# x loaded first from two queues, squares summed in pairs on TensorE, and the first block in halves

## The chip, the cores and the metric

The kernel runs on one NeuronCore of one Trainium2 chip. The metric is device time in microseconds (us), the median of three runs. The engines are TensorE (PE in the rows; PEld is its weight load), VectorE (DVE), ScalarE (ACT), GpSimd (POOL) and SyncE (SP), which here only issues transfers. SP's and ACT's transfers go through two queues, q1 and q10 in the rows, to the core's 16 DMA engines.

## The reference

One layer of a diffusion backbone on 256 prompt tokens and 1024 latent tokens of width 1024. Cut to what lies around the change:

```python
def rmsnorm(x, g):
    xf = x.astype(jnp.float32)
    r = lax.rsqrt(jnp.mean(xf * xf, axis=-1, keepdims=True) + EPS)
    return (xf * r).astype(x.dtype) * g

mod_ctx = (jax.nn.silu(c_ctx)[None] @ w_ada[i] + b_ada[i]).reshape(1, 1, N_MOD, D_MODEL)
mod_lat = (jax.nn.silu(c) @ w_ada[i] + b_ada[i]).reshape(c.shape[0], 1, N_MOD, D_MODEL)
...
h = rmsnorm(x, g_norm1) * (1.0 + scale_m) + shift_m
proj = h @ w_in
```

Behind that come a short convolution and a state-space mixer, an output projection, a second norm and a gated feed-forward block with a 3x3 convolution, and a final norm. All of it is in float32.

## The kernel before

Everything is held channel-major: x is 8 tiles of 128 channels (KT = 8), by 256 prompt columns (TP) and 1024 latent columns (TS). A float32 product of the projections is made of three fp32r products of a high and a low part (`hi`, `lo`; `whi`, `wlo`), which ScalarE and GpSimd or VectorE split.

The stage in question is the beginning, up to the first projection. SyncE issues the small constants (`sm`, `cst`, `rows`), then two prompt tiles `xp` (512 KB each, in pieces of 1 KB) and eight latent tiles `xs` (512 KB each, in pieces of 4 KB; they appear in the rows as `bcs` for k under 4 and as `x` for the others). ScalarE squares each tile, VectorE adds the squares up into one tile (`accp` for the prompt, `acc_s` for the latent tokens, both `bc` in the rows), and a matmul with a 128x128 tile of ones (`ones`) sums over the partitions into `pr_p` and `pr_s` (`yp` and `sa` in the rows). ScalarE makes the reciprocal roots `rp` and `rs` of them as exp(-0.5 ln(.)).

Meanwhile `ada_block(k)` computes shift and scale of the norm for the channels of tile k: a load of 1 MB of `w_ad1` into half of the buffer `xq` (`xs<-in_w_ad` in the rows), eight column-tiled matmuls with the silu of the conditioning (`sc`), a copy by ScalarE, two transposes, and three small VectorE instructions that end in `aff`. The loop over k then loads a weight block (`w_l`), calls `ada_block(k + 1)`, scales x (`stt(x, x, aff, rs)`), makes `hi` on ScalarE and `lo` on VectorE, and does twelve matmuls of 512 columns for the two projection blocks that are computed within the loop (`acc<-h` in the rows). The prompt's tiles are multiplied by `rp` and turned into `hp_hi` and `hp_lo` beside it.

The order on each engine is not the order of the code: a scheduler arranges the instructions of each engine by its own estimates, within the data dependencies, and `after(a, b)` adds an order by hand. A tile with a tag and a number of buffers (`T(pool, shape, tag, bufs)`) waits for the release of the buffer that it reuses; transfers share eight completion semaphores a queue's issuer waits on in turn.

Of the kernel before, what the change touches and what calls it, by code (L numbers as in the profile page):

```python
# [9 lines left out]
ALU = mybir.AluOpType  # L10
# [3 lines left out]
P = 128  # L14
# [41 lines left out]
def body(nc, tc, A):  # L56
    cnt = [0]

    def T(pool, shape, tag, bufs, dt=F32):
        cnt[0] += 1  # L60
        return pool.tile(list(shape), dt, tag=tag, bufs=bufs, name=f"{tag}_{cnt[0]}")
# [27 lines left out]

    sm = T(con, [P, SMW], "sm", 1)  # L90
    wff0, wff1 = SMO["wff"]
    dma(sm[:, wff1:], A["sm"][:, wff1:])
    dma(sm[:, 0:wff0], A["sm"][:, 0:wff0])
# [25 lines left out]
    g_hs, hsp = open_pool("hsp", side="right")  # L119
    g_cv, cv = open_pool("cv", side="right")  # L120
    g_xy, xy = open_pool("xy", side="right")
    g_sd, sd = open_pool("sd")
    g_w3, w3 = open_pool("w3")
    wx = [w3]
    g_nrm, nrm = open_pool("nrm")
# [13 lines left out]
    def psa():  # L139
        return T(ps, [P, 512], "sa", 3)  # L140
# [101 lines left out]
    xT = A["xT"]  # L242

    xp = [T(cv, [P, 4, TP], "xl", 2) for _ in range(2)]
    for q in range(2):
        dma(xp[q], xT[:, 4 * q:4 * q + 4, 0:TP])
# [9 lines left out]
    xs = [T(sd, [P, TS], "bcs", 4) if k < 4 else T(nrm, [P, TS], "x", 4) for k in range(KT)]  # L256
    acc_s = T(sd, [P, TS], "bc", 4)
    for k in range(KT):
        dma(xs[k], xT[:, k, TP:TT])
        q = T(cv, [P, TS], "cv", 4) if k else acc_s  # L260
        sq = act(q, xs[k], AF.Square)
        if k:
            tt(acc_s, acc_s, q, ALU.add)
    pr_s = [psa(), psa()]
    for i in range(2):
        nc.tensor.matmul(pr_s[i], ones, acc_s[:, i * 512:(i + 1) * 512], start=True, stop=True)
    tab = lnexp_table(sq)
    rp = T(cv, [P, TP], "cv", 4)
    rs = T(cv, [P, TS], "cv", 4)
    for r, a, b, src in ((rp, 0, TP, pr_p[:, 0:TP]), (rs, 0, 512, pr_s[0]), (rs, 512, TS, pr_s[1])):  # L270
        after(act(r[:, a:b], src, AF.Ln, scale=1.0 / D, bias=epsc), tab)
        act(r[:, a:b], r[:, a:b], AF.Exp, scale=-0.5)
# [43 lines left out]
    ada_block(0)  # L316
    for k in range(KT):
# [8 lines left out]
        stt(x, x, aff[:, 0, k, 1:2], rs, ALU.mult, ALU.mult)  # L326
        hi, lo = [T(hsp, [P, TS], "h", 16, F32R) for _ in range(2)]
        act(hi, x, AF.Identity, bias=col(0, k, 1))
# [11 lines left out]
        if i == 0:  # L340
            tt(xp[q], xp[q], rp.unsqueeze(1).broadcast_to([P, 4, TP]), ALU.mult)
# [995 lines left out]
```

## Time and profile before

| | |
|---|---|
| median of 3 runs | 1554.84 us (1553.34 to 1555.62) |
| the profiled run | 1553.6 us, its span 1551.8 us |
| TensorE busy | 1507.0 us, 97% of the span, 8724 matmuls |
| VectorE, ScalarE, GpSimd busy | 70%, 42%, 33% |
| mean granted TensorE clock | 0.996 of full speed |
| moved by DMA | 187.79 MB, 121 GB/s over the span |

The span runs from the first to the last instruction of the profiled execution; the time of a run lies about 2 us above it. A busy share is a mean over the whole span. The stage that the change touches is the first 75 us of it, and there the shares are others than in the table; the rows below are from this stage.

### The profile page before, as it was taken

Reading aid. Unit: us, or ns where it says so; the run is one execution under the profiler, and the core shown is the slowest. Engines: PE = TensorE matmul, PEld = TensorE weight load, DVE = VectorE, ACT = ScalarE, POOL = GpSimd, SP = SyncE. Lnnn points to the kernel's source line nnn. Section 1 sums busy time; section 2 is a strip of 40 time slices with the busy share of each in tenths; the row PEclk is TensorE's granted clock in tenths of the full one; section 3 lists DMA queues with packets and bytes.
Section 4 is the critical chain, followed back from the end, with each engine's and each line's share of the span. In section 5 each row is a group of like instructions: output and inputs, shape, how many; then the busy total and the mean of one; then the engine's idle time right before and its main releaser. Section 6 shows DMA issues by size and latency. Waiting matters only on the chain. (4 is left out here: it accounts for less than half of the span.)

```text
span 1551.8 us, 22546 instructions
## 1 busy us (share of the span) xinstructions
PE 1507.0 (97%) x8724; PEld 1289.1 (83%) x8724; DVE 1092.2 (70%) x1625; ACT 654.1 (42%) x1020; POOL 516.6 (33%) x289
## 2 busy tenths in 40 slices
PE   4999999999999999999999999999999999999997
PEld 2578888878788888888888888888888888888886
DVE  5765345287885467996666697556679978798696
ACT  6545334267775244433233342332334332433333
POOL 0432321111110003333333333333346554545452
PEclk9999999999999999999999999999999999999999
DMA  8635753443435513221222242121433323342221
GB/s 300 240 109 181 247 209 102 129 161 118 151 109 192 202 68 124 75 70 67 74 64 77 75 156 85 52 69 67 144 121 110 105 89 109 107 154 90 96 78 61
DMA packets 90653, 187.79 MB, mean 121 GB/s; under 512 B 9747, under 2 KB 37299, under 8 KB 90547
## 3 DMA queue, kind: packets, MB, share of 16 engines
q1 hardware_dynamic: 84722, 183.22, 35.0%
q10 hardware_dynamic: 5824, 3.15, 0.7%
q8 instruction: 68, 1.11, 0.3%
q14 instruction: 39, 0.31, 0.1%
HBM read 163.70 MB, written 22.63 MB: 120 GB/s over the span
## 5 line engine op out<-in xcount | busy, mean ns | idle before, releaser
L80 DVE SCALAR_TENSOR_TENSOR cc<-acc,sm,cc 128x504 f32<-128x504 f32 (+5 forms) x836 | 545.8, 665 | 111.3 <-ACT cc L1077 53.0
L77 POOL TENSOR_TENSOR wlo<-raw,whi 128x1024 fp32r<-128x1024 f32 (+2 forms) x91 | 212.6, 2336 | 637.8 <-ACT whi L157 554.0
L157 ACT ACTIVATE whi<-raw 128x1024 fp32r<-128x1024 f32 x97 | 102.6, 1057 | 238.4 <-PE acc L168 185.6
L80 DVE SCALAR_TENSOR_TENSOR x<-dn,mod,x 128x288 f32<-128x288 f32 (+2 forms) x176 | 96.1, 547 | 95.0 <-PE dn L170 94.5
L77 POOL TENSOR_TENSOR dlo<-draw,dhi 128x512 fp32r<-128x512 f32 (+1 forms) x88 | 108.8, 1237 | 89.6 <-ACT dhi L1130 89.6
L77 POOL TENSOR_TENSOR wlx<-raw,whx 128x1024 fp32r<-128x1024 f32 (+2 forms) x36 | 84.7, 2352 | 140.5 <-ACT whx L157 132.4
L168 PE MATMUL acc<-ya,whi 128*128 128x512 f32 (+1 forms) x400 | 118.8, 354 | 0.0
L166 PE MATMUL acc<-ya,whi 128*128 128x512 f32 (+1 forms) x400 | 118.7, 354 | 0.0
L170 PE MATMUL acc<-ya,wlo 128*128 128x512 f32 (+1 forms) x400 | 118.6, 354 | 0.0
L168 PE MATMUL acc<-oa,whi 128*128 128x512 f32 (+1 forms) x400 | 118.6, 354 | 0.0
L170 PE MATMUL acc<-oa,wlo 128*128 128x512 f32 (+1 forms) x400 | 118.6, 354 | 0.0
L166 PE MATMUL acc<-oa,whi 128*128 128x512 f32 (+1 forms) x400 | 118.2, 353 | 0.0
L166 PE MATMUL dn<-yb,dhi 128*128 128x288 f32 (+2 forms) x352 | 110.1, 313 | 5.6 <-DVE x L80 4.4
L168 PE MATMUL dn<-yb,dhi 128*128 128x288 f32 (+2 forms) x352 | 109.6, 311 | 0.8 <-POOL yb L77 0.8
L170 PE MATMUL dn<-yb,dlo 128*128 128x288 f32 (+2 forms) x352 | 109.4, 311 | 0.0
L166 PE MATMUL acc<-h,whi 128*128 128x512 f32 x336 | 108.0, 403 | 0.0
L170 PE MATMUL acc<-h,wlo 128*128 128x512 f32 x336 | 104.9, 394 | 0.0
L168 PE MATMUL acc<-h,whi 128*128 128x512 f32 x336 | 104.8, 393 | 0.0
L1130 ACT ACTIVATE dhi<-draw 128x512 fp32r<-128x512 f32 (+1 forms) x88 | 52.9, 602 | 121.3 <-PE dn L168 49.7
L166 PE MATMUL dn<-g,dhi 128*128 128x288 f32 (+2 forms) x304 | 95.1, 313 | 0.0
L168 PE MATMUL dn<-g,dhi 128*128 128x288 f32 (+2 forms) x304 | 94.8, 312 | 0.3 <-POOL g L77 0.3
L170 PE MATMUL dn<-g,dlo 128*128 128x288 f32 (+2 forms) x304 | 94.8, 312 | 0.0
(345 smaller groups left out, 3538.5 us busy)
## 6 DMA issues: line engine op xcount, KB each, us to landing
raw<-in_w_up SPq DMA_DIRECT2D x88, 512.0 KB, 3.3
raw<-in_w_in SPq DMA_DIRECT2D x32, 512.0 KB, 3.3
ws<-in_w_ada SPq DMA_DIRECT2D x64, 256.0 KB, 4.7
draw<-in_w_down SPq DMA_DIRECT2D x64, 256.0 KB, 2.8
xs<-in_w_ad SPq DMA_DIRECT2D x16, 512.0 KB, 4.5
bc<-csds SPq DMA_DIRECT2D x16, 512.0 KB, 3.6
raw<-in_w_out SPq DMA_DIRECT2D x16, 512.0 KB, 3.4
x<-in_xT SPq DMA_DIRECT2D x8, 640.0 KB, 8.1
```

The costliest lines, as they stand in the source:

```text
L77: (eng or V).tensor_tensor(out=out, in0=a, in1=b, op=op)
L80: V.scalar_tensor_tensor(out=out, in0=a, scalar=s, in1=b, op0=op0, op1=op1)
L157: act(hi, raw, AF.Copy)
L166: nc.tensor.matmul(o, wh[:, k, :], rh(k), start=k == 0, stop=False)
L168: nc.tensor.matmul(o, wh[:, k, :], rl(k), start=False, stop=False)
L170: mm = nc.tensor.matmul(o, wl[:, k, :], rh(k), start=False, stop=k == n - 1)
L1130: act(wh, raw, AF.Copy)
```

## The change

x is issued first: the two prompt tiles on ScalarE's queue, three latent tiles on SyncE's, then the part of `sm` with the conditioning, then the other five latent tiles, then the remaining constants. The pools that hold them are opened earlier for this. The squares of the latent tiles are no longer added up into one tile: each odd one is added to the even one ahead of it, and each of the four sums goes to TensorE, which adds them up in `pr_s`. The last pair's matmuls stand in the code behind `ada_block(0)`, with the roots behind them, and `rs` comes ahead of `rp`. In the loop's first turn (k = 0) the scaling of x and `hi` are done in two halves of 512 columns, and the prompt's multiplication by `rp` is put behind the second half.

```diff
--- before.py
+++ after.py
@@ -87,9 +87,25 @@
     g_wst, wst = open_pool("wst")
 
 
+    g_hs, hsp = open_pool("hsp", side="right")
+    g_cv, cv = open_pool("cv", side="right")
+    g_xy, xy = open_pool("xy", side="right")
+    g_sd, sd = open_pool("sd")
+    g_w3, w3 = open_pool("w3")
+    wx = [w3]
+    g_nrm, nrm = open_pool("nrm")
+    xT = A["xT"]
+    xp = [T(cv, [P, 4, TP], "xl", 2) for _ in range(2)]
+    for q in range(2):
+        nc.scalar.dma_start(xp[q], xT[:, 4 * q:4 * q + 4, 0:TP])
+    xs = [T(sd, [P, TS], "bcs", 4) if k < 4 else T(nrm, [P, TS], "x", 4) for k in range(KT)]
+    for k in range(3):
+        dma(xs[k], xT[:, k, TP:TT])
     sm = T(con, [P, SMW], "sm", 1)
     wff0, wff1 = SMO["wff"]
     dma(sm[:, wff1:], A["sm"][:, wff1:])
+    for k in range(3, KT):
+        dma(xs[k], xT[:, k, TP:TT])
     dma(sm[:, 0:wff0], A["sm"][:, 0:wff0])
 
     def smv(n):
@@ -116,13 +132,6 @@
     aff = T(con, [P, 2, KT, 2], "aff", 1)
 
 
-    g_hs, hsp = open_pool("hsp", side="right")
-    g_cv, cv = open_pool("cv", side="right")
-    g_xy, xy = open_pool("xy", side="right")
-    g_sd, sd = open_pool("sd")
-    g_w3, w3 = open_pool("w3")
-    wx = [w3]
-    g_nrm, nrm = open_pool("nrm")
     g_ps, ps = open_pool("ps1", space=PSUM)
 
     def pacc():
@@ -239,11 +248,7 @@
             after(ln, tab)
         return act(out, out, AF.Exp, scale=-0.5)
 
-    xT = A["xT"]
-
-    xp = [T(cv, [P, 4, TP], "xl", 2) for _ in range(2)]
-    for q in range(2):
-        dma(xp[q], xT[:, 4 * q:4 * q + 4, 0:TP])
+
     accp = T(sd, [P, 4, TP], "bc", 4)
     sqp = T(sd, [P, 4, TP], "bc", 4)
     act(accp, xp[0], AF.Square)
@@ -253,23 +258,17 @@
     pr_p = pst()
     for i in range(2):
         nc.tensor.matmul(pr_p[:, 0:TP], ones, accp[:, i], start=i == 0, stop=i == 1)
-    xs = [T(sd, [P, TS], "bcs", 4) if k < 4 else T(nrm, [P, TS], "x", 4) for k in range(KT)]
-    acc_s = T(sd, [P, TS], "bc", 4)
+    pr_s = [psa(), psa()]
     for k in range(KT):
-        dma(xs[k], xT[:, k, TP:TT])
-        q = T(cv, [P, TS], "cv", 4) if k else acc_s
+        q = T(cv, [P, TS], "cv", 4) if k % 2 else T(sd, [P, TS], "bc", 4)
         sq = act(q, xs[k], AF.Square)
-        if k:
-            tt(acc_s, acc_s, q, ALU.add)
-    pr_s = [psa(), psa()]
-    for i in range(2):
-        nc.tensor.matmul(pr_s[i], ones, acc_s[:, i * 512:(i + 1) * 512], start=True, stop=True)
-    tab = lnexp_table(sq)
-    rp = T(cv, [P, TP], "cv", 4)
-    rs = T(cv, [P, TS], "cv", 4)
-    for r, a, b, src in ((rp, 0, TP, pr_p[:, 0:TP]), (rs, 0, 512, pr_s[0]), (rs, 512, TS, pr_s[1])):
-        after(act(r[:, a:b], src, AF.Ln, scale=1.0 / D, bias=epsc), tab)
-        act(r[:, a:b], r[:, a:b], AF.Exp, scale=-0.5)
+        if k % 2 == 0:
+            qe = q
+            continue
+        tt(q, q, qe, ALU.add)
+        if k < KT - 1:
+            for i in range(2):
+                nc.tensor.matmul(pr_s[i], ones, q[:, i * 512:(i + 1) * 512], start=k == 1, stop=False)
     wdt = T(sd, [P, 640], "toks", 1)[:, 0:KT * 32].rearrange("p (k r) -> p k r", r=32)
     dma(wdt, A["w_dt"])
 
@@ -314,6 +313,14 @@
 
     pps = []
     ada_block(0)
+    for i in range(2):
+        nc.tensor.matmul(pr_s[i], ones, q[:, i * 512:(i + 1) * 512], start=False, stop=True)
+    tab = lnexp_table(sq)
+    rp = T(cv, [P, TP], "cv", 4)
+    rs = T(cv, [P, TS], "cv", 4)
+    for r, a, b, src in ((rs, 0, 512, pr_s[0]), (rs, 512, TS, pr_s[1]), (rp, 0, TP, pr_p[:, 0:TP])):
+        after(act(r[:, a:b], src, AF.Ln, scale=1.0 / D, bias=epsc), tab)
+        act(r[:, a:b], r[:, a:b], AF.Exp, scale=-0.5)
     for k in range(KT):
         raw = T(wst, [P, N_LOOP, P], "raw", 2)
         dma(raw, A["w_l"][k])
@@ -323,9 +330,12 @@
         if k < KT - 1:
             ada_block(k + 1)
         x = xs[k]
-        stt(x, x, aff[:, 0, k, 1:2], rs, ALU.mult, ALU.mult)
         hi, lo = [T(hsp, [P, TS], "h", 16, F32R) for _ in range(2)]
-        act(hi, x, AF.Identity, bias=col(0, k, 1))
+        for a in (0, 512) if k == 0 else (0,):
+            b = 512 + a if k == 0 else TS
+            first = V.scalar_tensor_tensor(out=x[:, a:b], in0=x[:, a:b], scalar=aff[:, 0, k, 1:2],
+                                           in1=rs[:, a:b], op0=ALU.mult, op1=ALU.mult)
+            act(hi[:, a:b], x[:, a:b], AF.Identity, bias=col(0, k, 1))
         stt(lo, x, col(0, k, 1), hi.bitcast(F32), ALU.add, ALU.subtract)
         hs_hi.append(hi)
         hs_lo.append(lo)
@@ -338,7 +348,8 @@
                                      start=k == 0 and n == 0, stop=k == KT - 1 and n == 2)
         q, i = k // 4, k % 4
         if i == 0:
-            tt(xp[q], xp[q], rp.unsqueeze(1).broadcast_to([P, 4, TP]), ALU.mult)
+            after(V.tensor_tensor(out=xp[q], in0=xp[q], in1=rp.unsqueeze(1).broadcast_to([P, 4, TP]),
+                                  op=ALU.mult), first)
         act(hp_hi[q][:, i], xp[q][:, i], AF.Identity, scale=aff[:, 0, k, 0:1], bias=col(0, k, 0))
         ts(xp[q][:, i], xp[q][:, i], aff[:, 0, k, 0:1], col(0, k, 0), ALU.mult, ALU.add)
         if k == 3:
```

How the order moves on the engines. On ScalarE, the beginning of the program; `xl` are the prompt tiles, `bcs` and `x` the latent ones, `sc` the silu, the words in brackets what the instruction waits for (`DMAHW` a transfer). Before:

```order
L114 ACT_TABLE_LOAD [waits DMAHW0_49]
L114 ACTIVATE sc_77<-sm_63 128x8x2 [waits DVE_49]
L110 ACT_TABLE_LOAD
L110 ACTIVATE arow_74<-rows_68 40x1 [waits DMAHW3_49]
L249 ACTIVATE bc_107<-xl_103 128x1024 [waits DMAHW4_49]
L250 ACTIVATE bc_108<-xl_104 128x1024 [waits DMAHW5_49]
L261 ACTIVATE bc_124<-bcs_116 128x1024 [waits DMAHW6_49]
L261 ACTIVATE cv_128<-bcs_117 128x1024 [waits DMAHW7_49]
```

and now:

```order
L100 DMA xl_81<-in_xT 128x4x256
L100 DMA xl_82<-in_xT 128x4x256
L254 ACT_TABLE_LOAD
L254 ACTIVATE bc_123<-xl_81 128x1024 [waits DMAHW0_49]
L255 ACTIVATE bc_124<-xl_82 128x1024 [waits DMAHW2_49]
L264 ACTIVATE bc_134<-bcs_85 128x1024 [waits DMAHW1_49]
L130 ACT_TABLE_LOAD [waits DMAHW5_49]
L130 ACTIVATE sc_115<-sm_96 128x8x2 [waits DVE_49]
L264 ACTIVATE cv_136<-bcs_86 128x1024 [waits DMAHW3_49]
L264 ACTIVATE bc_141<-bcs_87 128x1024 [waits DMAHW4_49]
```

The silu with its table load has moved from the front to behind the third square, and the prompt tiles' loads are on this engine.

On TensorE, from its first instruction to the transposes of block 0; `sa<-bc,ones` and `sa<-cv,ones` are the latent sums, `sa<-xs,sc` the modulation's matmuls. Before:

```order
L266 MATMUL sa_155<-bc_124,ones_70 128x512 [waits DVE_49]
L266 MATMUL sa_156<-bc_124,ones_70 128x512
L292 MATMUL sa_177<-xs_174,sc_77 32x256 [waits DMAHW7_49,Activation_49]
L292 MATMUL sa_177<-xs_174,sc_77 32x256 x3
L292 MATMUL sa_177<-xs_174,sc_77 32x256 [waits DMAHW0_49]
L292 MATMUL sa_177<-xs_174,sc_77 32x256 x3
L298 MATMUL yp_188<-cst_66,cv_186 128x128 [waits Activation_49]
```

and now:

```order
L271 MATMUL sa_132<-cv_136,ones_108 128x512 [waits DVE_49]
L271 MATMUL sa_133<-cv_136,ones_108 128x512
L271 MATMUL sa_132<-cv_143,ones_108 128x512 [waits DVE_49]
L271 MATMUL sa_133<-cv_143,ones_108 128x512
L271 MATMUL sa_132<-cv_150,ones_108 128x512 [waits DVE_49]
L271 MATMUL sa_133<-cv_150,ones_108 128x512
L317 MATMUL sa_132<-cv_157,ones_108 128x512 [waits DVE_49]
L317 MATMUL sa_133<-cv_157,ones_108 128x512
L291 MATMUL sa_169<-xs_166,sc_115 32x256 [waits DMAHW7_49,Activation_49]
L291 MATMUL sa_169<-xs_166,sc_115 32x256 x3
L291 MATMUL sa_169<-xs_166,sc_115 32x256 [waits DMAHW0_49]
L297 MATMUL yp_180<-cst_104,cv_178 128x128 [waits DMAHW4_49,Activation_49]
```

Two sums over 512 columns have become eight, and the last pair's (L317) stand ahead of the modulation's first block.

On VectorE, from block 0's reduction to x of k = 1. Before:

```order
L299 TENSOR_REDUCE mod_80<-yp_188 128x2x2 [waits PE_49]
L77 TENSOR_TENSOR mod_80<-mod_80,sm_63 128x2x2 [waits DMAHW0_49,DVE_49]
L83 TENSOR_SCALAR aff_81<-mod_80,sm_63 128x2 [waits DMAHW1_49,DVE_49]
L80 SCALAR_TENSOR_TENSOR bcs_116<-bcs_116,aff_81,cv_161 128x1024 [waits DMAHW6_49,DVE_49,Activation_49]
L299 TENSOR_REDUCE mod_80<-yp_213 128x2x2 [waits PE_49]
L83 TENSOR_SCALAR xl_103<-xl_103,aff_81,mod_80 128x256 [waits Activation_49]
L77 TENSOR_TENSOR mod_80<-mod_80,sm_63 128x2x2 [waits DVE_49]
L83 TENSOR_SCALAR aff_81<-mod_80,sm_63 128x2 [waits DVE_49]
L80 SCALAR_TENSOR_TENSOR bcs_117<-bcs_117,aff_81,cv_161 128x1024 [waits DMAHW7_49,DVE_49]
L80 SCALAR_TENSOR_TENSOR h_221<-bcs_116,mod_80,h_220 128x1024 [waits Activation_49]
```

and now:

```order
L298 TENSOR_REDUCE mod_118<-yp_180 128x2x2 [waits PE_49]
L77 TENSOR_TENSOR mod_118<-mod_118,sm_96 128x2x2 [waits DMAHW5_49,DVE_49]
L83 TENSOR_SCALAR aff_119<-mod_118,sm_96 128x2 [waits DMAHW3_49,DVE_49]
L336 SCALAR_TENSOR_TENSOR bcs_85<-bcs_85,aff_119,cv_190 128x512 [waits DMAHW1_49,DVE_49,Activation_49]
L298 TENSOR_REDUCE mod_118<-yp_216 128x2x2 [waits PE_49]
L336 SCALAR_TENSOR_TENSOR bcs_85<-bcs_85,aff_119,cv_190 128x512 [waits Activation_49]
L77 TENSOR_TENSOR mod_118<-mod_118,sm_96 128x2x2 [waits DVE_49]
L351 TENSOR_TENSOR xl_81<-xl_81,cv_189 128x1024 [waits DMAHW0_49,Activation_49]
L83 TENSOR_SCALAR aff_119<-mod_118,sm_96 128x2 [waits DVE_49]
L80 SCALAR_TENSOR_TENSOR h_223<-bcs_85,mod_118,h_222 128x1024 [waits Activation_49]
L83 TENSOR_SCALAR xl_81<-xl_81,aff_119,mod_118 128x256 [waits Activation_49]
L336 SCALAR_TENSOR_TENSOR bcs_86<-bcs_86,aff_119,cv_190 128x1024 [waits DVE_49]
```

The first block's scaling is in two halves with the reduction of block 1 between them, and the prompt's multiplication (`xl<-xl,cv`) stands ahead of `aff` of block 1.

## Rows read from the trace of the kernel before

**Rows 1.** The page: the span and the line of the busy times (busy us, share of the span, instructions).
```profile
span 1551.8 us, 22546 instructions
...
PE 1507.0 (97%) x8724; PEld 1289.1 (83%) x8724; DVE 1092.2 (70%) x1625; ACT 654.1 (42%) x1020; POOL 516.6 (33%) x289
```

**Rows 2.** The timeline of SyncE's issues: start us, length us, queue, line, what is issued, how many.
```profile
0.74 0.39 SPq L92 DMA_DIRECT2D sm<-in_sm  x1
...
2.58 0.95 SPq L246 DMA_DIRECT2D xl<-in_xT  x2
3.57 2.16 SPq L259 DMA_DIRECT2D bcs<-in_xT  x4
5.77 2.57 SPq L259 DMA_DIRECT2D x<-in_xT  x4
```

**Rows 3.** ScalarE's timeline in the first 30 us: start us, length us, engine, line, operation, out<-in, count, and in brackets the idle time ahead and what ended it.
```profile
2.58 1.28 ACT L114 ACT_TABLE_LOAD   x1 [2.58 <-DMA sm<-in_sm]
3.88 0.22 ACT L114 ACTIVATE sc<-sm 128x16 f32<-128x16 f32 x1
...
6.56 1.06 ACT L249 ACTIVATE bc<-xl 128x1024 f32<-128x1024 f32 x1 [0.95 <-DMA xl<-in_xT]
8.02 1.06 ACT L250 ACTIVATE bc<-xl 128x1024 f32<-128x1024 f32 x1 [0.40 <-DMA xl<-in_xT]
9.40 1.06 ACT L261 ACTIVATE bc<-bcs 128x1024 f32<-128x1024 f32 x1 [0.33 <-DMA bcs<-in_xT]
...
18.46 1.06 ACT L261 ACTIVATE cv<-x 128x1024 f32<-128x1024 f32 x1 [0.26 <-DMA x<-in_xT]
19.54 1.28 ACT L225 ACT_TABLE_LOAD   x1
...
25.55 0.63 ACT L272 ACTIVATE cv<-cv 128x512 f32<-128x512 f32 x1
26.09 0.37 ACT L295 ACTIVATE cv<-sa 128x256 f32<-128x256 f32 x1
...
29.67 1.15 ACT L328 ACTIVATE h<-bcs,mod 128x1024 fp32r<-128x1024 f32 x1 [0.77 <-DVE bcs L80]
```

**Rows 4.** VectorE's timeline in the first 32 us, with the same columns.
```profile
11.77 9.21 DVE L77 TENSOR_TENSOR bc<-bc,cv 128x1024 f32<-128x1024 f32 x7 [0.71 <-ACT cv L261]
21.79 2.89 DVE L77 TENSOR_TENSOR xl<-xl,cv 128x1024 f32<-128x1024 f32 x2 [0.81 <-ACT cv L272]
27.04 0.17 DVE L299 TENSOR_REDUCE mod<-yp 128x4 f32<-128x16 f32 x1 [2.37 <-PE yp L298]
...
28.36 1.28 DVE L80 SCALAR_TENSOR_TENSOR bcs<-bcs,aff,cv 128x1024 f32<-128x1024 f32 x1
29.56 0.17 DVE L299 TENSOR_REDUCE mod<-yp 128x4 f32<-128x16 f32 x1
29.64 0.40 DVE L83 TENSOR_SCALAR xl<-xl,aff,mod 128x256 f32<-128x256 f32 x1
...
30.15 0.23 DVE L83 TENSOR_SCALAR aff<-mod,sm 128x2 f32<-128x2 f32 x1
30.42 1.28 DVE L80 SCALAR_TENSOR_TENSOR bcs<-bcs,aff,cv 128x1024 f32<-128x1024 f32 x1
```

**Rows 5.** TensorE's timeline: the prompt's sum, the latent sums, the modulation's first matmuls, the first matmuls of k = 0 and of k = 1, and the first instruction behind the loop. A float32 matmul of the code is two instructions here.
```profile
11.11 2.07 PE L255 MATMUL yp<-bc,ones 128*128 128x256 f32 x4 [11.11 <-DVE bc L77]
21.03 3.76 PE L266 MATMUL sa<-bc,ones 128*128 128x512 f32 x4 [7.85 <-DVE bc L77]
24.72 1.91 PE L292 MATMUL sa<-xs,sc 128*32 128x256 f32 x26
...
30.88 1.61 PE L337 MATMUL acc<-h,whi 128*128 128x512 f32 x4 [1.62 <-ACT h L328]
...
36.65 1.17 PE L337 MATMUL acc<-h,whi 128*128 128x512 f32 x4
...
72.95 1.07 PE L311 MATMUL sa<-xl,toks 128*32 128x256 f32 x16
```

**Rows 6.** The durations in ns (least, median, most) of the `ones` matmuls, at L266 in this stage and at L235 in later norms.
```profile
L266 PE MATMUL sa<-bc,ones x4: 1041/1061/1223, 21.0 to 23.8; 128*128 128x512 f32 x4
...
L235 PE MATMUL dn<-nacc,ones x10: 325/592/636, 560.5 to 1350.3; 128*128 128x512 f32 x6, 128*128 128x256 f32 x2, 128*128 128x192 f32 x2
```

**Rows 7.** Stretches of the span: us, then busy us (instructions) of PE, PEld, DVE, ACT and POOL, the granted TensorE clock, the DMA share and GB/s.
```profile
10.00:20.00 10.00, 2.07 (x4) 1.17 (x4) 8.62 (x9) 8.32 (x9) 0.00 (x0) 1.00 1.03 408
...
28.00:31.40 3.40, 1.60 (x12) 0.83 (x13) 3.24 (x7) 2.25 (x4) 0.24 (x1) 1.00 0.89 316
31.40:34.90 3.50, 3.50 (x15) 1.42 (x15) 3.01 (x4) 1.54 (x2) 0.00 (x0) 0.51 0.92 332
...
40.00:50.00 10.00, 9.12 (x58) 5.29 (x49) 8.38 (x12) 4.09 (x9) 5.61 (x3) 1.00 0.66 237
50.00:60.00 10.00, 9.97 (x73) 5.61 (x72) 6.18 (x12) 4.88 (x8) 2.26 (x2) 1.00 0.72 253
60.00:70.00 10.00, 10.00 (x55) 5.01 (x53) 7.34 (x9) 6.03 (x8) 5.15 (x3) 1.00 0.52 182
```

**Rows 8.** ScalarE's issue of a store to `zd` (timeline), then the DMA queues' packets, MB and share of 16 engines in two stretches: 79.6 to 81.0 us, where q1 is the only queue that moved anything, and 108.8 to 109.4 us, where q1 loads in pieces of 2 KB and q10 stores in pieces of 512 bytes.
```profile
78.47 0.40 ACTq L445 DMA_DIRECT2D zd<-xl  x1
...
q1 hardware_dynamic: 94, 0.39, 85.9%
...
q1 hardware_dynamic: 78, 0.14, 86.2%
q10 hardware_dynamic: 120, 0.06, 32.6%
```

## The prediction

> **What bounds the kernel now.** I read the page first. TensorE is busy for 97% of the span [rows 1], so what the change does in the first 70 us reaches the end only as the moment at which TensorE gets into its steady run. TensorE does nothing until 11.11 us, works 2 us for the prompt's sum, waits until 21.03 us for the squares of the latent tokens, and enters the loop over k at 30.88 us [rows 5]. From 36.65 us, the first matmul of k = 1, it is busy nearly without a gap: 9.12 of 10 us, 9.97 of 10 and 10.00 of 10 in the next stretches [rows 7], and at 72.95 us the loop is over [rows 5]. Nothing behind that is changed. So the question is how far the start of k = 1 and the few gaps behind it move, and that shift goes to the end one to one.
>
> The views by engine say what sets this start. SyncE spends its first four issues on small constants, and the first part of x is issued at 2.58 us [rows 2]. The transfers then fill the wires: 408 GB/s at a share of 1.03 from 10 to 20 us [rows 7]. ScalarE squares each tile as it lands: the first at 6.56 us, the second at 8.02, the third at 9.40, the last from 18.46 to 19.52 us, each taking 1.06 us while the tiles come about 1.28 us apart [rows 3]; it is paced by the data. VectorE adds them up (1.23 us each, 9.21 us for seven [rows 4]), TensorE sums over the partitions with `ones` from 21.03 to 24.72 us [rows 5], and then block 0 of the modulation follows. I call the end of the last `ones` matmul T: T = 24.72 us before.
>
> **The change, part by part.** *Earlier issue.* The first of x is issued at 0.74 instead of 2.58 us, so the whole train of ten 512 KB tiles can be 1.84 us earlier. The wires were full behind it, so this is a shift and not more bandwidth: unshared, the first tile lands at 6.56 − 1.84 = 4.7 us, each further tile 1.28 us later, the last near 16.6 us instead of 18.46. The second queue in itself brings no bandwidth, since one queue moved 408 GB/s [rows 7]. The Trainium skill, "DMA: Bandwidth & Descriptors", section "Issuing engines are not separate DMA queues", says the same, that a second issuing engine saves issue time alone; by that rule the gain of this part is the 1.84 us at most, and the trace agrees.
>
> *What ScalarE then waits for.* Its first two squares are those of the two prompt tiles, now alone on ScalarE's own queue, in 1 KB pieces against 4 KB pieces on SyncE's. How do two busy queues share? The nearest rows are where ScalarE stores to `zd` while SyncE loads. From 79.6 to 81.0 us SyncE's queue had all the packets although a store had been issued at 78.47 us; from 108.8 to 109.4 us, with pieces again in the ratio 1:4, ScalarE's queue moved 0.06 MB beside 0.14 MB [rows 8], three tenths of the bytes. By three tenths the second prompt tile lands when 6.7 tiles in all have been moved: 4.7 + 5.7 × 1.28 = 12.0 us. By a third (six tiles) it is 11.1, by equal bytes (four tiles) 8.6, and had ScalarE's queue the wires alone, 8.02 − 1.84 = 6.2 us. I take 11.5, between the two that are nearest to the row, and keep 6.2 and 12.0.
>
> *Silu's table.* The table load and the silu (1.28 + 0.22 us [rows 3]) lay in the wait for x. Now they stand behind the third square and wait for `sm`, which is behind three tiles of x on its queue. They are paid in the row of squares. ScalarE is no longer paced by data but by itself: from the landing of the second prompt tile, two squares, table and silu, seven squares, 2 × 1.06 + 1.50 + 7 × 1.06 = 11.0 us. With 11.5 the last square ends at 22.5 us, 3 us later than before. With the early landing `sm` decides instead: five tiles and 54 KB ahead, 4.7 + 4 × 1.28 + 0.13 = 9.95, then 1.50 + 7 × 1.06, which ends at 18.9.
>
> *Pairs for TensorE.* VectorE loses seven adds of which the last alone was exposed and gains four of the same size, again with one exposed (1.23 us), so it gives nothing back. TensorE's sums grow from two 512-column products to eight, each of two instructions. Their price depends on the clock. The clock column shows full speed up to 31.40 us [rows 7], but the durations say otherwise: a 128x512 instruction took 1061 ns here and 592 ns for the same form later [rows 6]; the level of 1.2 GHz until 24.72, of 2.4 GHz after. So a pair (four instructions) costs 3.69 us at the low level [rows 5], and 4 × (1061 − 592 = 469) ns less, some 1.8 us, at the high one; I use 3.6 and 1.7 with the fill hidden. Before, the level rose after 3.7 us of unbroken work. The Trainium skill, "TensorE: Matmul & The Clock Gate", section "Part 1: The HAM clock gate", says that the throttled clock is the default and activity lifts it; the 1061 against 592 ns agree. I therefore let pair 1 run low and pairs 2 to 4 high. Pair 1 is ready after two squares, table and silu, one square and an add: 2 × 1.06 + 1.50 + 1.06 + 1.3 = 6.0 us after the second prompt tile. From there TensorE is the limit, since later pairs are ready every 2.1 us: T = landing + 6.0 + 3.6 + 3 × 1.7 = landing + 14.7. With 11.5: **T = 26.2, 1.5 us later**. With the bounds: 12.0 gives 26.7; 8.6 gives 23.3; where `sm` decides, 9.95 + 1.50 + 1.06 + 1.3 + 3.6 + 5.1 = 22.5. T is unchanged for a landing at 10.0 us.
>
> *Modulation's first block ahead of the last pair.* In the program's order it is not: the two matmuls of L317 stand before all of L291's on TensorE. Nothing of it is hidden.
>
> *From T to k = 1.* ScalarE copies block 0's result at 26.09, 1.4 us after T, in the kernel before, held up by the exponentials [rows 3]; now the copy goes first, about T + 1.1 (call it C), and both logarithms and exponentials of `rs`, then those of `rp` and a weight conversion, stand between it and the copy of block 1. At 0.3 us for the copies and the small ones and 0.55 for 512 columns this copy ends about C + 4.0. The transposes (0.44) and the reduction (0.17) follow, C + 4.7. That reduction stands on VectorE ahead of the second half of x's first block, so the halving brings the first four matmuls only. Behind it VectorE does the half (0.7), an add (0.2), the prompt's multiplication, which was done at 21.79 while VectorE was idle (1.22), aff (0.25), the low part of h (1.2), 0.45, x of k = 1 (1.2): C + 9.95. ScalarE's h of k = 1 takes 1.15: C + 11.15, TensorE T + 12.3. Before: 36.65 − 24.72 = T + 11.9 [rows 4, 5]. So +0.4 us here, although the half clock of 31.40 to 34.90 us [rows 7] had slowed the old start. By my count of the blocks k = 1 to 3 the VectorE chain of about 4.6 us a block then makes some 2 us of small gaps where before there were 1.3, while TensorE has by then 0.8 us less of k = 0 left: +0.4 − 0.1 = **+0.3 us**. Bounds: −0.5 if the clock stays high, +2 if its low stretch falls on block 0's eight remaining matmuls (1.85 us of work at the high level) in place of the waits ahead of them.
>
> **The sum.** +1.5 + 0.3 = +1.8 us. The profiled run took 1553.6 us, span 1551.8 [rows 1], so 1555.4 for such a run; its time was 1.2 us below the median of 1554.84, so I forecast **1556.6 us** for the median.
>
> **The rivals.** *Slower, clock late or low again.* If the level has not risen when pair 2 starts, that pair costs 1.9 us more (T = 28.1); if the low stretch later hits block 0, +1.7 more. One of them gives +3.7 (1558.5), both +5.4 (1560.2). For it: TensorE's clock did fall in this stretch, 0.51 from 31.40 to 34.90 us [rows 7], and between C + 1 and C + 8 it has little work. Against it: pair 1 alone is about as much unbroken work as the one that lifted the clock before. It decides when pair 2 still runs at over a microsecond an instruction.
>
> *Faster: the prompt tiles land early.* If ScalarE's queue gets half of the bytes or more, T = 23.3 or 22.5, −1.4 to −2.2; with the +0.3, about −1.5 (1553.3), with a kind clock −2.7 (1552.1). For it: both queues start empty, unlike in [rows 8], where SyncE's was full when the store came. Against it: the 30% there. It decides at a landing of the second prompt tile before 10.0 us.
>
> *Nothing moves.* The loop could absorb any start, if its own transfers set its pace: its weights arrive at about 240 GB/s there, far from full [rows 7], and TensorE is nearly gapless, so I hold this for unlikely; it would give 1554.8.
>
> **How the numbers follow.** My case: 0.45, own range 1555.2 to 1558.2. Late clock: 0.2. Early prompt tiles: 0.3. Nothing: 0.05. The range 1552.6 to 1559.8 leaves out the better half of the fast case's kind clock and the two late clocks together. A measurement of this kernel tells about 0.2%, 3.1 us: under 1551.7 lies a fifth of the early case, 0.06; above 1557.95 lie nearly all of the late clocks and some of my own case, 0.22; within, 0.72.
>
> **What would show it.** In the changed kernel's profile: the first x issued near 0.74 us; a wait of ScalarE for the second prompt tile until 11 or 12 us, then squares 1.06 us apart without waits; the table load in their midst; pair 1 at over 1 us an instruction and pair 4 at 0.6; T near 26; the first matmul of k = 1 twelve microseconds behind it; the loop's end 1 to 3 us behind 72.95. I am wrong if the prompt tiles land before 10 us, if the pairs stay slow, or if the loop ends where it did although T moved.

## The result and the profile after

The changed kernel took 1560.77 us (median of 9 runs, 1557.17 to 1563.09), the kernel before 1554.84 beside it (nine runs too, of which one, at 3548.57 us, stays out of the ratio). The ratio is 1.0035, interval 1.0027 to 1.0044: slower by about 5.4 us, by the medians 5.9. I had forecast 1556.6 us, 1.8 us more, which is less than a measurement of this kernel can tell, with a range that ended at 1559.8. The time went the way I said and three times as far. The profiled execution took 1557.32 us, one of the shortest of its nine. All pages and timelines below have the columns of the rows of before. The page after:

```profile
span 1555.5 us, 22563 instructions
...
PE 1513.5 (97%) x8736; PEld 1291.8 (83%) x8736; DVE 1088.9 (70%) x1623; ACT 652.7 (42%) x1021; POOL 517.3 (33%) x289
```

The span is 3.7 us longer than in [rows 1]. ScalarE's timeline of the changed kernel, which answers to [rows 3]:

```profile
5.97 1.06 ACT L254 ACTIVATE bc<-xl 128x1024 f32<-128x1024 f32 x1 [2.90 <-DMA xl<-in_xT]
11.55 1.06 ACT L255 ACTIVATE bc<-xl 128x1024 f32<-128x1024 f32 x1 [4.52 <-DMA xl<-in_xT]
...
13.57 1.28 ACT L130 ACT_TABLE_LOAD   x1
14.86 0.22 ACT L130 ACTIVATE sc<-sm 128x16 f32<-128x16 f32 x1
...
20.66 1.04 ACT L264 ACTIVATE cv<-x 128x1024 f32<-128x1024 f32 x1
...
27.28 0.38 ACT L294 ACTIVATE cv<-sa 128x256 f32<-128x256 f32 x1 [3.75 <-PE sa L291]
...
29.74 0.48 ACT L322 ACTIVATE cv<-yp,epsc 128x256 f32<-128x256 f32 x1
...
31.33 0.38 ACT L294 ACTIVATE cv<-sa 128x256 f32<-128x256 f32 x1 [0.35 <-PE sa L291]
...
37.48 1.15 ACT L338 ACTIVATE h<-bcs,mod 128x1024 fp32r<-128x1024 f32 x1 [0.77 <-DVE bcs L336]
```

The first x is issued at 0.73 us. The second prompt tile is squared at 11.55 us, after a wait of 4.52; the table load and the silu stand in the row of squares; the last square ends at 21.7. Block 0's result is copied at 27.28, block 1's at 31.33, and between them stand both parts of `rs` and then `rp` (29.74). TensorE's timeline, which answers to [rows 5]:

```profile
14.64 2.07 PE L260 MATMUL yp<-bc,ones 128*128 128x256 f32 x4 [14.64 <-DVE bc L77]
17.34 7.16 PE L271 MATMUL sa<-cv,ones 128*128 128x512 f32 x12 [0.62 <-DVE cv L77]
24.33 1.88 PE L317 MATMUL sa<-cv,ones 128*128 128x512 f32 x4
26.14 1.07 PE L291 MATMUL sa<-xs,sc 128*32 128x256 f32 x16
...
30.27 0.44 PE L297 MATMUL yp<-cst,cv 128*128 128x128 f32 x2 [1.51 <-ACT cv L322]
...
33.45 0.73 PE L347 MATMUL acc<-h,whi 128*128 128x512 f32 x2 [0.68 <-ACT h L338]
...
39.22 1.19 PE L347 MATMUL acc<-h,whi 128*128 128x512 f32 x4
...
75.44 1.07 PE L310 MATMUL sa<-xl,toks 128*32 128x256 f32 x16
```

T is 26.14 (24.72 before), k = 1 begins at 39.22 = T + 13.1 (T + 11.9 before), and the loop ends at 75.44 (72.95). Note the transposes of block 0 at 30.27: they waited for L322, the logarithm of `rp`. VectorE's timeline, to [rows 4]:

```profile
30.75 0.17 DVE L298 TENSOR_REDUCE mod<-yp 128x4 f32<-128x16 f32 x1 [7.35 <-PE yp L297]
...
33.38 1.22 DVE L351 TENSOR_TENSOR xl<-xl,cv 128x1024 f32<-128x1024 f32 x1
...
36.16 1.28 DVE L336 SCALAR_TENSOR_TENSOR bcs<-bcs,aff,cv 128x1024 f32<-128x1024 f32 x1
```

VectorE idles 7.35 us ahead of block 0's reduction. The first of the prompt's two multiplications, which [rows 4] has at 21.79 in idle time, now stands between the two halves of k = 0 and x of k = 1 (36.16, before 30.42).

### The profile page after: what moved, and what is told of

Read it like the earlier page. It is cut to its first block, busy times and chain, and to the rows that moved or that the text cites. A ratio compares the mean times of both kernels' runs of the same rounds, so it can differ in the third digit from the quotient of the medians.

```text
span 1555.5 us, 22563 instructions
## 1 busy us (share of the span) xinstructions
PE 1513.5 (97%) x8736; PEld 1291.8 (83%) x8736; DVE 1088.9 (70%) x1623; ACT 652.7 (42%) x1021; POOL 517.3 (33%) x289
## 5 line engine op out<-in xcount | busy, mean ns | idle before, releaser
L77 POOL TENSOR_TENSOR dlo<-draw,dhi 128x512 fp32r<-128x512 f32 (+1 forms) x88 | 108.8, 1237 | 89.3 <-ACT dhi L1141 89.2
L179 PE MATMUL dn<-yb,dlo 128*128 128x288 f32 (+2 forms) x352 | 109.4, 311 | 0.0
```

Of the source, the lines that this page charges most:

```text
L77: (eng or V).tensor_tensor(out=out, in0=a, in1=b, op=op)
L179: mm = nc.tensor.matmul(o, wl[:, k, :], rh(k), start=False, stop=k == n - 1)
```

## The experiments

In the table T is the start of the matmuls behind the last `ones`, "k1" the first matmul of k = 1 less T, "half" the number of stretches of about 3.4 us at half clock before 80 us, M the start of `sa` from mod and toks, the first matmuls behind the loop's own. All from one profile each; the ratio is that of the timed runs, with its interval, to the kernel before timed beside them.

| kernel | T | k1 | half | M | median us | ratio to before |
|---|---|---|---|---|---|---|
| before, three profiles | 24.72, 25.21, 24.84 | 11.9, 11.3, 11.3 | 1, 0, 0 | 73.8, 73.7, 73.3 | 1554.0 to 1554.8 | |
| after, four profiles | 26.14, 26.97, 26.02, 26.16 | 13.1, 13.8, 15.0, 15.0 | 0, 1, 2, 2 | 76.3, 77.7, 77.8, 78.0 | 1560.77, 1560.46 | 1.0035 [1.0027, 1.0044], 1.0042 [1.0027, 1.0057] |
| e1_one_queue | 21.40 | 15.5 | 2 | 73.8 | 1553.81 | 0.9996 [0.9987, 1.0005] |
| e2_silu_first | 25.19 | 15.0 | 2 | 76.8 | 1557.18 | 1.0027 [1.0016, 1.0039] |
| e3_both | 21.14 | 13.1 | 0 | 71.1 | 1552.18 | 0.9993 [0.9984, 1.0002] |
| e4_pairs_alone | 23.83 | 10.5 | 0 | 72.2 | 1553.06 | 1.0000 [0.9991, 1.0009] |
| e5_rp_first | 26.27 | 12.0 | 1 | 76.3 | 1558.45 | 1.0026 [1.0016, 1.0035] |
| e6_whole_block | 26.38 | 16.4 | 2 | 79.9 | 1562.35 | 1.0051 [1.0039, 1.0064] |
| e7_tail_undone | 26.84 | 13.9 | 2 | 78.9 | 1558.50 | 1.0029 [1.0017, 1.0040] |
| e8_head_kept | 21.34 | 12.6 | 1 | 72.4 | 1553.89 | 0.9998 [0.9989, 1.0008] |
| e9_rp_before_block | 27.01 | 11.0 | 1 | 76.0 | 1556.99 | 1.0014 [1.0004, 1.0024] |
| e10_both_rp | 21.79 | 10.7 | 0 | 70.2 | 1552.78 | 0.9992 [0.9981, 1.0003] |
| e11_loads_only | 23.26 | 10.7 | 0 | 71.7 | 1553.66 | 0.9993 [0.9985, 1.0002] |

**The queue of the prompt's pieces.** e1_one_queue is the changed kernel with one line changed:

```
-        nc.scalar.dma_start(xp[q], xT[:, 4 * q:4 * q + 4, 0:TP])
+        dma(xp[q], xT[:, 4 * q:4 * q + 4, 0:TP])
```

> The changed kernel with the two prompt tiles issued by SyncE ahead of the latent ones, so one queue carries all of x. Theory 1 (the prompt tiles, sharing with SyncE's queue, hold up ScalarE's squares): the second prompt tile lands near 6.2 us instead of 11.55, the last square ends near 17.7 us, the last ones matmul (T) near 21 us instead of 26.1, and the loop ends some 5 us earlier than in the changed kernel, 2 to 3 us earlier than before; time 1552 to 1553 where before takes 1554.8. Rival (the loop is paced by its own loads, or by the order behind T): T moves but the loop's end stays within 1 us of the changed kernel's 75.4 us, time 1559 to 1561.

e2_silu_first is the changed kernel with the small table `sm` put back ahead of x, e3_both has both edits:

```
+    sm = T(con, [P, SMW], "sm", 1)
+    wff0, wff1 = SMO["wff"]
+    dma(sm[:, wff1:], A["sm"][:, wff1:])
     xp = [T(cv, [P, 4, TP], "xl", 2) for _ in range(2)]
...
```

> The changed kernel with the part of sm that the silu needs issued first, ahead of all of x; the prompt tiles stay on ScalarE's queue. Theory 1: the second prompt tile still lands at 11.5 to 12 us, the table load and silu go back into the wait ahead of the first square, and T comes 1.5 us earlier (24.7 us); time 1.5 us below the changed kernel. Rival (the prompt tiles cost nothing, the table load alone does): the squares end near 18.5 us and T is near 22 us, 4 us below the changed kernel.

> Both of these edits: sm first, then all of x on SyncE's queue. Theory 1: no stall of ScalarE but for data, T near 21.2 us, the same as with one queue alone within 0.5 us, since there the table load falls into slack; time 1552 to 1553. Rival (the order behind T, with the halves and the prompt's multiplication, is what costs): the loop ends near 73 to 75 us in spite of a T of 21, time 1555 to 1559.

ScalarE's timeline of e1:

```profile
4.54 1.06 ACT L254 ACTIVATE bc<-xl 128x1024 f32<-128x1024 f32 x1 [2.52 <-DMA xl<-in_xT]
6.00 1.06 ACT L255 ACTIVATE bc<-xl 128x1024 f32<-128x1024 f32 x1 [0.41 <-DMA xl<-in_xT]
```

On one queue the prompt tiles are squared at 4.54 and 6.00 us instead of 5.97 and 11.55, and T falls by 4.6 to 5.6 us. The small table first saves about 1 us of T alone (25.19) and 0.3 with one queue (21.14). From e2 to e3 only the queue differs: 4.05 us in T, 5.0 in the median, with ratios whose intervals lie apart. Not all of the 5.0 is T: the way from T to k = 1 is 1.9 us longer in e2, whose profile has two stretches at half clock there, where that of e3 has none. So the second queue is what makes T late, and a late T reaches the end. With T some 3.4 us earlier than in the kernel before, though, e1 is no shorter than that kernel: the order behind T, which e1 keeps, and two stretches at half clock eat it (T to k = 1 takes 15.5 us).

**Pairs alone, loads alone.** e4_pairs_alone is the kernel before with the sums in pairs, e11_loads_only the kernel before with all loads of x right behind the first small table:

```
-        q = T(cv, [P, TS], "cv", 4) if k else acc_s
+        q = T(cv, [P, TS], "cv", 4) if k % 2 else T(sd, [P, TS], "bc", 4)
...
+        for i in range(2):
+            nc.tensor.matmul(pr_s[i], ones, q[:, i * 512:(i + 1) * 512], start=k == 1, stop=k == KT - 1)
```

```
     dma(sm[:, wff1:], A["sm"][:, wff1:])
...
+    for q in range(2):
+        dma(xp[q], xT[:, 4 * q:4 * q + 4, 0:TP])
...
+    for k in range(KT):
+        dma(xs[k], xT[:, k, TP:TT])
```

> The kernel before with nothing changed but the sums in pairs (each pair's sum goes to TensorE, all four added in PSUM). Theory 1, with the clock's level lifted by the first pairs: the last square still ends at 19.5 us, the last pair takes 1.8 us instead of 3.7, T is near 22.7 us instead of 24.7 and the whole is 2 us below before (1552.8). Rival (the low clock stays through all pairs): the four pairs run end to end at 3.6 us each, T near 29, 4 us above before.

> The kernel before with one thing alone: all loads of x stand right behind the first small table, on SyncE's queue; squares, sums and everything behind them as before. The last square should end at 18.1 as in the runs with this queue order, T at 21.5 (at full clock) to 23.2 (at half), 1.5 to 3.2 us earlier than in the kernel before. If the end follows T: median 1551.2 to 1553. If an earlier T is given back behind it: 1553.5 to 1554.5.

Neither is slower, neither measurably faster. Pairs alone bring T forward by 1.1 us, where 2.0 were expected, and cost nothing that can be measured. The early loads bring M about 2 us forward, and the median only by 0.35, inside the interval.

**The order behind T, put back piece by piece.** e5_rp_first:

```
-    for r, a, b, src in ((rs, 0, 512, pr_s[0]), (rs, 512, TS, pr_s[1]), (rp, 0, TP, pr_p[:, 0:TP])):
+    for r, a, b, src in ((rp, 0, TP, pr_p[:, 0:TP]), (rs, 0, 512, pr_s[0]), (rs, 512, TS, pr_s[1])):
```

> The changed kernel with one thing put back: the prompt tile's root (logarithm and exponential of rp) stands ahead of the two halves of rs again. Theory A (the order behind T is what was mis-sized): in the changed kernel block 0's transposes start at 30.27, 4.1 us behind T (the end of the last `ones` matmul, 26.14), because their accumulator tile has one buffer, which holds the prompt's sum of squares until rp's logarithm has read it; with rp first they start 1.5 to 2 us behind T, the square roots still end at the same time, so the multiplication of k = 0 and with it everything behind comes 1 to 2 us earlier: the loop's end to `sa` from mod and toks is 50.2 - 1.5 = 48.5 to 49.2 us behind T, and the median 1558.5 to 1560. Theory B (the clock falls more often in the changed kernel, the order costs nothing): the distance stays 50.2 unless a stretch at half clock falls in it, and the median stays 1560 to 1561.

e6_whole_block undoes the halves and the order of the prompt's multiplication:

```
+        stt(x, x, aff[:, 0, k, 1:2], rs, ALU.mult, ALU.mult)
...
-        for a in (0, 512) if k == 0 else (0,):
...
+        act(hi, x, AF.Identity, bias=col(0, k, 1))
...
-            after(V.tensor_tensor(out=xp[q], in0=xp[q], in1=rp.unsqueeze(1).broadcast_to([P, 4, TP]),
-                                  op=ALU.mult), first)
+            tt(xp[q], xp[q], rp.unsqueeze(1).broadcast_to([P, 4, TP]), ALU.mult)
```

> The changed kernel with the first block of k = 0 whole again (one multiplication of 1024 columns and one copy to the high part) and the prompt's multiplication no longer ordered behind the first half; rs still ahead of rp. Theory A: the wait of block 0's transposes for rp's logarithm stays (transposes 4.1 us behind T), and VectorE, idle until they are through, does both prompt multiplications (1.22 us each) in that gap or right behind it, so that the halves' order is worth between a gain of 1 us and a loss of 1.5 us: median 1559.5 to 1562. If instead the halves are what costs (two starts, and the copy of each half), the median falls to 1558 to 1559 although the transposes still start 4.1 us behind T. Theory B: median 1560 to 1561.

e7_tail_undone has all code behind the squares as in the kernel before (last pair in the loop, roots right behind it with `rp` first, then block 0), e8_head_kept the same with `sm` first and one queue:

```
-        if k < KT - 1:
-            for i in range(2):
-                nc.tensor.matmul(pr_s[i], ones, q[:, i * 512:(i + 1) * 512], start=k == 1, stop=False)
+        for i in range(2):
+            nc.tensor.matmul(pr_s[i], ones, q[:, i * 512:(i + 1) * 512], start=k == 1, stop=k == KT - 1)
+    tab = lnexp_table(sq)
...
+    for r, a, b, src in ((rp, 0, TP, pr_p[:, 0:TP]), (rs, 0, 512, pr_s[0]), (rs, 512, TS, pr_s[1])):
...
```

> The changed kernel's first part (x first, the prompt's pieces on ScalarE's queue, pairs added by TensorE) with everything behind the squares as in the kernel before: the last pair in the loop, the roots right behind it with rp first, then block 0, the first block of x whole. T should stay at 25.5 to 26.2. Theory A: T to the start of `sa` from mod and toks is 47.3 to 48.5 us where no stretch at half clock falls in it (50.2 in the changed kernel), so the median is that of the kernel before plus the 1.4 us of T, and up to 1 more: 1555.5 to 1557.5. Theory B: the order is worth nothing, and the median stays at 1560 to 1561.

> Small table first, then all of x on SyncE's queue, pairs added by TensorE, everything behind the squares as in the kernel before. Theory A: T at 21.1 as in the run of both halves undone, and 47.3 to 48.5 from T to `sa` from mod and toks without a stretch at half clock, so 3 to 3.5 us under the kernel before in a run with equal clock: median 1550 to 1551.5 beside 1554.2, a ratio of 0.9975 to 0.9985. Theory B: no better than the run with the changed order behind T (1552.2).

TensorE's timeline of e5, block 0's transposes:

```profile
28.21 0.44 PE L297 MATMUL yp<-cst,cv 128*128 128x128 f32 x2 [0.87 <-ACT cv L322]
```

e5 did what was expected of the transposes (T + 1.9, in the changed kernel T + 4.1). Its median is 2.0 to 2.3 us lower, about as expected, but the intervals of the two ratios overlap; with one stretch at half clock, k = 1 came at T + 12.0, in the changed kernel at T + 13.8. The distance from T to M, forecast at 48.5 to 49.2, was 50.0 with a stretch at half clock in it. e6 came out higher than the change, again with overlapping intervals, and with two stretches at half clock its k = 1 came at T + 16.4, in the changed kernel at T + 15.0: in this order the halves, or the place of the prompt's multiplication, seem to help. e7 and e8 missed: the source order of before does not give the order of before, because the scheduler now places block 1 elsewhere. ScalarE's timeline of e7:

```profile
28.89 0.36 ACT L299 ACTIVATE cv<-sa 128x256 f32<-128x256 f32 x1
...
31.82 1.15 ACT L332 ACTIVATE h<-bcs,mod 128x1024 fp32r<-128x1024 f32 x1 [0.77 <-DVE bcs L80]
32.88 0.36 ACT L299 ACTIVATE cv<-sa 128x256 f32<-128x256 f32 x1
```

Block 1's copy stands behind h of k = 0, T + 6.0, and its transposes come at T + 7.2; in the kernel before they came at 28.06, T + 3.3. So e7 and e8 test another order, not the old one, and tell little on the question.

**The prompt's root ahead of block 0.** ScalarE and VectorE are idle from 23.5 to 27.3 and 30.7 us in the changed kernel. e9_rp_before_block puts `rp` and both prompt multiplications there and leaves all else of the change; e10_both_rp does so in e3_both.

```
...
+    after(act(rp, pr_p[:, 0:TP], AF.Ln, scale=1.0 / D, bias=epsc), tab)
+    act(rp, rp, AF.Exp, scale=-0.5)
+    for xq_ in xp:
+        tt(xq_, xq_, rp.unsqueeze(1).broadcast_to([P, 4, TP]), ALU.mult)
     ada_block(0)
...
-    for r, a, b, src in ((rs, 0, 512, pr_s[0]), (rs, 512, TS, pr_s[1]), (rp, 0, TP, pr_p[:, 0:TP])):
+    for r, a, b, src in ((rs, 0, 512, pr_s[0]), (rs, 512, TS, pr_s[1])):
...
-        if i == 0:
-            after(V.tensor_tensor(out=xp[q], in0=xp[q], in1=rp.unsqueeze(1).broadcast_to([P, 4, TP]),
-                                  op=ALU.mult), first)
```

> The changed kernel with the prompt's root (logarithm and exponential of rp) and both prompt multiplications ahead of block 0, so that they run in the idle time of ScalarE and VectorE ahead of T; last pair, rs and halves stay as changed. If the wait of block 0's transposes for rp's logarithm and the prompt's multiplication between the blocks of VectorE are what the changed order costs: T at 26.1, transposes of block 0 at T + 1.9 (in the changed kernel T + 4.1), first matmul of k = 1 at T + 10 to 11.5 (T + 13.1), median 1557 to 1558.5. If the order is not it, T + 13 and 1560 to 1561; with rp put first alone it was 1558.45.

> The same tail (prompt's root and multiplications ahead of block 0) with the small table first and all of x on SyncE's queue. If the end follows T and the distance behind it one for one: T at 21.1, first matmul of k = 1 at T + 10 to 11.5, median 1550 to 1551.5 beside 1554.4 of the kernel before, the first version under both. If an earlier T is given back behind it (more idle time or more half clock, as the run with the first part kept and the old source order behind it suggests: T 3.4 us earlier, time 0.5 us shorter), 1552.5 to 1554.

TensorE's timeline of e9, behind its T of 27.01:

```profile
28.59 0.44 PE L297 MATMUL yp<-cst,cv 128*128 128x128 f32 x2 [0.51 <-ACT cv L294]
...
31.87 0.73 PE L351 MATMUL acc<-h,whi 128*128 128x512 f32 x2 [1.85 <-ACT h L342]
...
38.01 0.73 PE L351 MATMUL acc<-h,whi 128*128 128x512 f32 x2
```

The wait for the logarithm is gone (transposes at T + 1.6, in the changed kernel T + 4.1), and k = 1 begins at T + 11.0 although a stretch at half clock falls there; with one, the changed order took 13.8 and the order before 11.9. The median falls by 3.5 us, and the intervals lie apart. What is left against the kernel before, a ratio of 1.0014 or 2.2 us, is about what T is later in these profiles, 2.1 us. In e10 T and the distance are both short, M is 3.1 to 3.6 us under the kernel before's, and yet its median of 1552.78 is 1.2 us under it, inside the interval. It is far below the changed kernel, and no version measurably beats the kernel before.

**Both kernels again.** The same two files, for more profiles.

> The changed kernel itself once more, for a second profile: the first one's own time (1557.32) lies 3.4 us under the median of its runs, and no stretch at half clock falls in its first 80 us, where the kernel before has one (31.5 to 34.9). Theory A (late order, and besides it a first stretch at half clock in most executions): one or two such stretches between 27 and 40, and the `sa` matmuls from mod and toks start at 77 to 79 instead of 76.3. Theory B (the order behind T alone): no stretch there again, 76.3, and what lifts the median lies behind 80 us. Median 1559.5 to 1561 either way.

> The changed kernel, a third profile. Its first two were executions with a mean granted clock of 0.996 (two stretches at half clock each), 3.4 and 1.5 us under the medians, while most of its executions show 0.994. Theory A (the order behind T costs about 2.4 us whatever the clock does, and most executions have one or two further stretches at half clock): the first matmul of k = 1 at T + 13.1 to 13.8, and at a clock of 0.994 four stretches, each of them worth 1.2 to 1.7 us. Theory C (the median lies higher for a wait that the first two profiles do not show): the same two stretches, and a wait of 1.5 to 3.4 us at a new place.

> The changed kernel, a fourth profile, with the expectations of the third.

> The kernel before, a second profile. Theory A: T at 24.7 as before, and the first matmul of k = 1 at T + 11.9 if a stretch at half clock falls between 25 and 36 again, at T + 10.5 to 11 if none does; 1551.5 to 1555.

> The kernel before, a third profile, with the expectations of the second.

The stretches of a_third, with the columns of [rows 7]:

```profile
27.00:30.00 3.00, 1.14 (x14) 0.38 (x10) 0.00 (x0) 2.84 (x6) 0.00 (x0) 1.00 0.76 261
31.00:37.00 6.00, 5.52 (x25) 1.80 (x22) 5.71 (x10) 2.92 (x5) 0.66 (x1) 0.50 0.85 286
```

the same two of the first profile of the changed kernel:

```profile
27.00:30.00 3.00, 1.26 (x14) 0.38 (x10) 0.00 (x0) 2.72 (x6) 0.00 (x0) 1.00 0.73 249
31.00:37.00 6.00, 4.82 (x32) 2.11 (x27) 5.88 (x11) 3.62 (x7) 0.93 (x2) 1.00 0.87 274
```

and the six microseconds of b_third, the kernel before:

```profile
31.00:37.00 6.00, 5.08 (x28) 3.47 (x29) 4.93 (x9) 3.19 (x5) 0.70 (x1) 1.00 0.98 369
```

In a_third TensorE works 1.14 of 3 us while it waits for block 0, and then its clock is at half (1.2 of 2.4 GHz) for two stretches on end, on the matmuls of k = 0 and block 2. The first profile has nearly the same wait, 1.26 of 3 us, and full clock behind it, so the wait alone does not decide. With the changed order k = 1 came at T + 13.08, 13.08 (after, e3) without a stretch at half clock, 13.77 with one, and 14.95, 14.96, 14.97, 15.5 with two (a_fourth, a_third, e2, e1). With the old order it came at 11.27 and 11.29 without, 11.93 with one. Theory C (a new wait) falls: a_third and a_fourth show no wait that the first profile lacks, but a slower clock. My expectation that an execution at a granted clock of 0.994 has four such stretches held (two at 30 to 38, two near 970). Their price at the start was below what I expected, 0.65 to 1.2 us each.

## Why the prediction was wrong

**The sum by stages**, means of four profiles after and three before: T 26.32 against 24.92, **+1.4**; from T to k = 1, 14.19 against 11.50, **+2.7**; from k = 1 to M, 36.94 against 37.18, **−0.2**; from M to the last `acc` matmul, 1468.0 against 1466.5, **+1.5**. Together +5.4, the measured ratio. My sum had +1.5, +0.3 with the gaps behind k = 1, and nothing.

- *T* was right, in size and in its steps: the second prompt tile at 11.55 (forecast 11.5), the last square's end at 21.7 (22.5), T at 26.1 (26.2). Pair 1 ran at the low clock, the last pair at the high one: 592 ns an instruction. Part of it was luck: the share I took from [rows 8] was three tenths, while the queues' rows (last section) show four tenths from 1 to 6 us and a quarter from 6 to 11, and only the two together (1.05 of 3.33 MB) make three tenths.
- ***From T to k = 1* is the step that failed**: +0.4 us in my chain, +2.7 measured, in three pieces. First, the order costs 1.8 us at full clock (13.1 against 11.3), where my chain gave T + 12.3. The two stretches from T to k = 1, of the first profile after and of b_third, with the columns of [rows 7]:

```profile
26.14:39.22 13.08, 9.89 (x78) 4.47 (x77) 8.09 (x17) 8.94 (x18) 2.19 (x3) 1.00 0.78 258
```

```profile
24.84:36.13 11.29, 9.12 (x69) 4.69 (x69) 7.01 (x12) 6.70 (x12) 1.41 (x2) 1.00 0.86 301
```

  TensorE idles 3.2 us instead of 2.2 and works 9.9 instead of 9.1. ScalarE's part of my chain held: h of k = 1 ends at 38.63, T + 12.5. But TensorE was last: it had idled 1.5 us for `yp`, worked without a gap from 33.45, and the new order has 58 of the blocks' matmuls between T and k = 1 where the old one had 50; the last ten of them fill it up to k = 1. The tile `yp` has one buffer, which holds the prompt's sum until `rp`'s logarithm has read it. I followed block 1's copy through the new order and not block 0's transposes, which seemed free once their copy came first. e5, which shortens this wait, and e9, which removes it (and moves the prompt's multiplication too), show it. Second, the baseline: T + 11.9 holds a stretch at half clock that two further profiles of the same kernel do not have, so I compared with a distance 0.65 too long. Third, the clock: three of four profiles after have one or two stretches at half clock there, a price of 0.7 to 1.9 us. I had that price as my upper bound (+2) and as half of the slower rival, with a chance of 0.2. The timed runs agree with the profiles: their mean granted clock was 0.9943 and 0.9944 with the change (9 and 5 runs), 0.9953 to 0.9959 for the kernel before (21 to 30 runs in each group). What brings these stretches on was not tested by itself and stays open; e9, without the wait, still had one.
- *The rival "late or low clock"* came nearest: 1558.5 to 1560.2, by another mechanism in its larger part. *Early prompt tiles* was refuted by the row at 11.55, and e1 shows that it would have taken one queue to get them. *Nothing moves* was refuted for a later start, by e2 against e3; an earlier start than before was mostly given back (M 2.5 us earlier in e3, 3.4 in e10, and no measurable time).
- *"Nothing behind that is changed, and that shift goes to the end one to one"* is true of the order of instructions, which is the same on each engine behind the loop, and not of the time. I put this term at nothing, and it was +1.5. Matmul by matmul against the mean of the three profiles before, 1.3, 1.3, 2.2 and 2.1 us came between 785 and 1470 us: 0.5 to 1.6 at the wait near 967 us, the rest in two steps of some 0.35 us near 1211 and 1466 (the two steps do not show in e2 to e7). TensorE's timeline at the wait near 967 us, of the kernel before and then of the changed kernel's first profile:

```profile
966.90 0.74 PE L166 MATMUL dn<-yb,dhi 128*128 128x448 f32 x1 [3.00 <-DVE x L80]
```

```profile
969.90 0.74 PE L175 MATMUL dn<-yb,dhi 128*128 128x448 f32 x1 [3.66 <-DVE x L80]
```

The wait there was 3.00 to 3.01 us in all three profiles before, 3.35 to 3.87 after, and in a_third and a_fourth two stretches at half clock follow it instead of one. The other kernels waited 2.77 to 4.04 us. e10 lost 2.7 us of its early start between 785 and 1470 us too, and e11 some 2.5 us by 250, where its profile has a stretch at half clock between 230 and 240. Why these places answer to a change of the start is left open.

## What to carry to other kernels

Before a root, a copy or a reduction is moved in a queue, list the buffers that it frees as well as the values that it makes: a single PSUM buffer that waits for a late reader holds up everything that comes next in that buffer. An engine's idle time ahead of the point that sets the end is the place for work that needs nothing late (here the prompt's root), and when two queues are busy, look at the size of their pieces: here pieces of a quarter of the size got about a quarter of the other queue's bytes, so the data that is wanted first should not be the small pieces. (Larger pieces on the second queue were not tried.) When a baseline term comes from one profile, ask whether it holds a stretch at a lower clock, and compare at equal clock.

## What the runs showed of the hardware

*How two busy queues share.* The DMA queues of the changed kernel from 7.0 to 7.5 us, q1 with pieces of 4 KB, q10 with pieces of 1 KB (queue, packets, MB, share of 16 engines):

```profile
q1 hardware_dynamic: 41, 0.16, 81.5%
q10 hardware_dynamic: 37, 0.04, 21.4%
```

They went nearly one packet for one packet, so the smaller pieces got 0.04 of 0.20 MB. The Trainium skill, "DMA: Bandwidth & Descriptors", section "Queues, rings and completion order", says that each DMA engine takes the queues that have work in turn, a packet at a time; the trace agrees, 41 to 37 by the profile's count of packets. Over 6 to 11 us it was 0.49 of 1.93 MB, a quarter, less than the three tenths of [rows 8]. From 1 to 6 us the second queue had more:

```profile
q1 hardware_dynamic: 220, 0.84, 53.1%
q10 hardware_dynamic: 563, 0.56, 31.7%
```

That is 0.56 of 1.40 MB, two thirds of it from 4 to 5 us, when q1 moved only 0.01 MB. So the landing came out as forecast all the same.

*Half clock.* The stretches at half clock lasted about 3.4 us each, singly or two on end: at the start and near 230 or 400 us in some profiles, and near 970 in every profile of every kernel, there behind the longest wait that TensorE has after its start (2.77 to 4.04 us). The same file had none or one (before), none, one or two (after) at its start. In the rows before 25 us the clock column reads 1.00 while the durations are those of the low level (1061 ns in [rows 6]); the column alone would have hidden it.
